# Hybrid delta-rule encoder on one core: the first norm's squares added in pairs on VectorE, layer 2 tiles from token 14, the scan's record in the inverse's tile, query-key blocks one tile sooner

## The chip, the cores and the metric

The kernel runs on one core of one Trainium2 chip. The metric is the device time of one execution in microseconds (us), lower is better. An execution takes 2422.28 us before the change (median of 3 runs, 2419.74 to 2425.08).

## The reference

Two layers of a hybrid encoder over 1040 tokens (16 learned meta tokens ahead of 1024 inputs) of width 1024, all in float32. The meta tokens are dropped at the end, so the second layer's outputs are only wanted from token 16 on.

```python
def hybrid_mixer(h, w_in, conv_qkv_w, a_log, dt_bias, dn_norm_w, sc_conv_w, w_out):
    proj = h @ w_in.astype(h.dtype)
    qkv, z, b_raw, a_raw, sc_b, sc_c, sc_h = jnp.split(proj, idx, axis=-1)
    qkv = jax.nn.silu(depthwise_conv_centred(qkv, conv_qkv_w))
    ...
    q = l2norm(q.reshape(Bsz, L, DN_HEADS, DN_HEAD_DIM))
    k = l2norm(k.reshape(Bsz, L, DN_HEADS, DN_HEAD_DIM))
    ...
    o_fwd = chunk_gated_delta_rule(qp, kp, vp, gp[:, :, 0], bp[:, :, 0])
    o_bwd = flip(chunk_gated_delta_rule(flip(qp), flip(kp), flip(vp),
                                        flip(gp[:, :, 1]), flip(bp[:, :, 1])))
    o = (o_fwd + o_bwd)[:, N_PAD:]
    ...
    y_sc = sc_b * depthwise_conv_centred(sc_c * sc_h, sc_conv_w)
    mix = jnp.concatenate([o, y_sc], axis=-1)
    return mix @ w_out.astype(h.dtype)

for l in range(DEPTH):
    h = h + hybrid_mixer(rmsnorm(h, norm1_w[l]), w_in[l], ...)
    h = h + swiglu(rmsnorm(h, norm2_w[l]), w_gate_up[l], w_down[l])
h = rmsnorm(h, final_norm_w)
return h[:, N_META:]
```

Each delta-rule group (4 heads of 128) needs, for each chunk and direction, the inverse of a unit triangular matrix made of key-key products and decays, a query-key block times the same decays, and then a scan over the chunks that carries a 128x128 state per head. The convolutions have three taps (one token to either side).

## The kernel before

**Layout.** The activations lie transposed: 128 channels on the partitions, tokens along the free axis. A projection of 1024 channels to a tile of 128 channels (`dense`) is 8 steps in k, and each step is three products, because an fp32 operand is held as a rounded high part and a low part: high x high (L169), high weight x low input (L170), low weight x high input (L171). The 1040 tokens go in three chunks of 348, 346 and 346, so a tile of 128 channels is 3 x 24 products; each chunk has a PSUM bank of its own and is evacuated by VectorE (L333 with the norm's factor `rstd` multiplied in, L338 as a plain copy). Weights come by DMA as `raw`, ScalarE makes the high part `whi` (L138), VectorE the low part `wlo` (L139).

**Order.** The program's order on each engine is set by a scheduler from priorities: the dense products of a layer run through, and small jobs are queued (`jobs`, `jobs2`, `jobs3`), of which one each is issued behind every chunk of 24 products. The tensor engine (PE) therefore sees a nearly unbroken row of dense products with small products let in between. "Dense product number n" below counts L169, L170 and L171 from the start of the program.

**First norm.** The squares of the 8 input tiles `hv` are summed over the partitions by products with a matrix of ones, column-tiled: four products of 128x32 with 260 tokens each lie side by side in one bank `fps` (L287). There are 8 x 4 of them, one set for each input tile. The root (L222), its reciprocal (L223) and two DMAs through DRAM (`rsd`, then `rstd` spread over the partitions) follow. The first two tiles of keys are evacuated before `rstd` is there, as copies, and multiplied later (L797).

**Attention of a layer.** In order: four key tiles (each: projection, convolution, silu, square, and a sum of squares over the channels by products with `sel`, L736), then the query tiles, the gates (L389, L426), the decays, which go to DRAM as `dtd` (L519), the key-key products, and the substitution that inverts 32x32 blocks (`sub_start`, `substitute`, in a tile with the halves `W` and `X`, VectorE L607 and L608). Then come four value tiles and, alternating, tiles of the short convolution (`sc_tile`) and of the output gate (`z_tile`). During those, `jobs2` holds `chunk_a` for each chunk: the query-key products (L573), two loads of decays `dt` from DRAM (issued by ScalarE's queue, L576), two multiplications on VectorE (L577), and two writes to `aqd` (L578, SP's queue). The `dt` tiles are from a ring of five buffers. The query-key banks are two. `jobs3` holds `invert`, which joins the 32x32 inverses to 128x128 ones in five rounds, `first` to `fifth` (L652 to L713). The fourth reads `W` last, the fifth reads `X` last.

**Scan.** Two directions run interleaved, each with a record of values `V`, keys `K`, query-key blocks `A` and gate `sz`, loaded from DRAM by SP's queue (L927 to L930; for the meta tokens L1008 and L1026). The record `rec` (L907) is a tile of its own that takes the buffer of the inverse's tile:

```python
rec = sb.tile([128, 4 * L], F32, tag=Y[0][2], name=nm("rec"))
```

Then come the output projection, the second norm and the feed-forward part (2816 channels), which take the rest of a layer's time.

## Time and profile before

| quantity | value |
|---|---|
| median of 3 runs | 2422.28 us |
| profiled execution, its own time | 2422.37 us |
| its span on the core | 2420.6 us |
| VectorE (DVE) busy | 1829.9 us |
| ScalarE (ACT) busy | 1045.7 us |
| GpSimd (POOL) busy | 70.3 us |
| mean DMA rate over the span | 139 GB/s |

The span runs from the first to the last recorded instruction; 1.8 us of the run's own time lie outside it. In the rows below, the first number is the start in us from the span's start and the second the busy time; "x8" counts instructions, and a bracket holds the idle time of the engine ahead of the row with what ended it. A product in float32 that is 32 columns wide, or one of 128x128, is recorded as two matmul records.

### The profile page before, as it was taken

The page shows a single profiled execution, that of the slowest core. Times are in us where ns is not written, and L with a number is a line of the kernel's source. Part 1 is how long each engine was busy: PE and PEld are TensorE (multiplying, and loading weights), DVE is VectorE, ACT ScalarE, POOL GpSimd, SP SyncE. Part 2 cuts the span into 40 slices and gives each one's busy share as a digit, 9 for nine tenths or more (in the row PEclk, how much of TensorE's full clock was granted, in tenths as well). Part 3 has the DMA queues.
Part 4 walks back from the last instruction along what each step waited for, and adds up shares of the span by engine and source line. Part 5 has one row for each costly group of instructions (what it writes and reads, how often), then busy time and mean ns, then how long its engine had stood idle before and what let it go on. Part 6 is the DMA issues. An engine that isn't in the chain of part 4 may idle for free.

```text
span 2420.6 us, 44960 instructions
## 1 busy us (share of the span) xinstructions
PE 2403.1 (99%) x17559; PEld 2228.1 (92%) x17559; DVE 1829.9 (76%) x3320; ACT 1045.7 (43%) x1977; POOL 70.3 (3%) x157
## 2 busy tenths in 40 slices
PE   9999999999999999999999999999999999999998
PEld 8999999999999999999999998998988888888887
DVE  6797545769888877977657985457898887778875
ACT  6653234446233333444446532335653343334444
POOL 0140000000000000000000200000000000000002
PEclk9999999999999999999999999999999999999999
DMA  4545344634222224674224444446433232347641
GB/s 136 158 154 187 119 154 150 206 111 132 93 97 89 102 74 136 224 246 148 89 84 151 154 154 145 147 144 222 142 114 113 77 112 85 121 144 249 204 127 70
DMA packets 202637, 336.60 MB, mean 139 GB/s; under 512 B 23488, under 2 KB 89208, under 8 KB 202424
## 3 DMA queue, kind: packets, MB, share of 16 engines
q1 hardware_dynamic: 174600, 295.12, 36.5%
q10 hardware_dynamic: 25648, 34.24, 4.3%
q0 software_dynamic: 2176, 4.36, 0.6%
q8 instruction: 138, 2.26, 0.4%
q14 instruction: 75, 0.61, 0.1%
HBM read 251.52 MB, written 82.12 MB: 138 GB/s over the span
## 4 chain that ended last, share of the span: by engine, by line
PE 95%; DMA 2%; DVE 2%; ACT 1%; SPq 0%; issue 0%; DVEq 0%; ACTq 0%
PE pacc L169 11%; PE pacc L170 11%; PE pacc L171 11%; PE pacc L1240 4%; PE pacc L1244 4%; PE pacc L1243 4%; PE pb L1244 3%; PE pb L1240 3%; PE pb L1243 3%; PE pf L940 3%; PE pf L1240 3%; PE pf L1244 3%; PE pf L1243 3%; PE pb L940 3%; PE pacc L1808 2%; PE pacc L1807 2%
## 5 line engine op out<-in xcount | busy, mean ns | idle before, releaser
L169 PE MATMUL pacc<-a,whi 128*128 128x346 f32 (+1 forms) x800 | 259.8, 325 | 0.6 <-ACT a L190 0.3
L171 PE MATMUL pacc<-a,wlo 128*128 128x346 f32 (+1 forms) x800 | 259.5, 326 | 0.2
L169 PE MATMUL pacc<-b,whi 128*128 128x346 f32 (+2 forms) x672 | 232.1, 346 | 0.4 <-ACT b L1124 0.3
L171 PE MATMUL pacc<-b,wlo 128*128 128x346 f32 (+2 forms) x672 | 231.6, 347 | 0.0
L138 ACT ACTIVATE whi<-raw 128x512 fp32r<-128x512 f32 x166 | 104.2, 630 | 285.0 <-PE pacc L170 206.3
L170 PE MATMUL pacc<-a,whi 128*128 128x346 f32 (+1 forms) x681 | 221.4, 325 | 0.6 <-DVE a L191 0.6
L170 PE MATMUL pacc<-b,whi 128*128 128x346 f32 (+2 forms) x580 | 199.4, 344 | 0.0
L169 PEld LDWEIGHTS pacc<-a,whi 128*128 128x128 f32 x800 | 151.0, 189 | 2.7 <-issue 1.1
L171 PEld LDWEIGHTS pacc<-a,wlo 128*128 128x128 f32 x800 | 150.8, 189 | 2.2 <-issue 1.3
L139 DVE TENSOR_TENSOR wlo<-raw,whi 128x512 fp32r<-128x512 f32 x166 | 113.8, 687 | 45.4 <-ACT whi L138 44.7
L169 PEld LDWEIGHTS pacc<-b,whi 128*128 128x128 f32 x672 | 126.3, 188 | 11.0 <-issue 1.3
L171 PEld LDWEIGHTS pacc<-b,wlo 128*128 128x128 f32 x672 | 126.1, 188 | 10.1 <-issue 2.3
L170 PEld LDWEIGHTS pacc<-a,whi 128*128 128x128 f32 x681 | 128.6, 189 | 3.8 <-issue 1.5
L170 PEld LDWEIGHTS pacc<-b,whi 128*128 128x128 f32 x580 | 109.1, 188 | 6.6 <-issue 0.6
L1222 ACT ACTIVATE whi<-rw 128x512 fp32r<-128x512 f32 (+1 forms) x84 | 51.7, 620 | 105.9 <-PE pacc L1243 27.4
L1222 ACT ACTIVATE b<-rw 128x512 fp32r<-128x512 f32 (+1 forms) x63 | 38.7, 620 | 89.2 <-PE pb L1243 34.5
L1222 ACT ACTIVATE a<-rw 128x512 fp32r<-128x512 f32 (+1 forms) x63 | 38.5, 619 | 71.9 <-PE pacc L1243 33.1
L1223 DVE TENSOR_TENSOR wlo<-rw,whi 128x512 fp32r<-128x512 f32 (+1 forms) x84 | 56.2, 671 | 6.5 <-ACT whi L1222 6.1
L333 DVE TENSOR_TENSOR a<-pacc,rstd 128x346 f32<-128x346 f32 (+2 forms) x59 | 32.6, 553 | 36.7 <-PE pacc L171 34.3
L1808 PE MATMUL pacc<-P,wlo 128*128 128x260 f32 (+1 forms) x177 | 59.4, 336 | 0.0
L1805 PE MATMUL pacc<-P,whi 128*128 128x260 f32 (+1 forms) x177 | 59.4, 336 | 0.0
L1807 PE MATMUL pacc<-P,whi 128*128 128x260 f32 (+1 forms) x177 | 59.4, 336 | 0.0
(1160 smaller groups left out, 7844.0 us busy)
## 6 DMA issues: line engine op xcount, KB each, us to landing
raw<-in_w_in SPq DMA_DIRECT2D x110, 256.0 KB
raw<-in_w_gu SPq DMA_DIRECT2D x106, 256.0 KB
rw<-in_w_gu SPq DMA_DIRECT2D x90, 256.0 KB
rw<-in_w_dn SPq DMA_DIRECT2D x90, 192.0 KB
rec<-vkd SPq DMA_DIRECT2D x61, 256.0 KB
raw<-in_w_out SPq DMA_DIRECT2D x48, 256.0 KB
b<-ad SPq DMA_DIRECT2D x45, 260.0 KB
a<-ad SPq DMA_DIRECT2D x45, 256.0 KB
```

The costliest lines, as they stand in the source:

```text
L138: whi_done[0] = hasten(wpr, lambda: act(out=hi, in_=raw[:, 0:kk, :], func=AF.Copy))
L139: whi_done[1] = hasten(wpr, lambda: tt(out=lo, in0=raw[:, 0:kk, :], in1=hi.bitcast(F32), op=ALU.subtract))
L169: mm(ps[:, :n], wh, xh[:, n0:n1], start=(i == 0), stop=False)
L170: mm(ps[:, :n], wh, xl[:, n0:n1], start=False, stop=False)
L171: last_mm[0] = mm(ps[:, :n], wl, xh[:, n0:n1], start=False, stop=(i == K - 1))
L940: one = mm(*args, **kw)
L1222: hasten(wpr, lambda: act(out=hi, in_=src, func=AF.Copy))
L1240: one = mm(ps[:, :CW], w[0][:, k, :], th[:, cs], start=first and k == 0, stop=False, skip_group_check=True)
L1243: mm(ps[:, :CW], w[0][:, k, :], tl[:, cs], start=False, stop=False, skip_group_check=True)
L1244: one = mm(ps[:, :CW], w[1][:, k, :], th[:, cs], start=False, stop=stop and k == nk - 1, skip_group_check=True)
L1807: mm(ps[:, :CW], wh[:, k, :], tl[:, cs], start=False, stop=False, skip_group_check=True)
L1808: mm(ps[:, :CW], wl[:, k, :], th[:, cs], start=False, stop=en, skip_group_check=True)
```

## The change

Four places change.

1. **First norm.** Each of four squares (ScalarE) gets a second one added to it (two of them squared by VectorE, two by ScalarE; the addition on VectorE), so four sets of column-tiled products are left instead of eight. The tie that held a set until its neighbour's squares were there goes.
2. **Layer 2 from token 14.** The query tiles and the first two parts of the short-convolution tiles are projected, convolved and multiplied from token 14 on, in three chunks of 342 (`near`). The squares of the query tiles are set to zero ahead of token 14 by GpSimd.
3. **The record lies in the inverse's tile by parts**, with the directions' halves exchanged, so a load into `W`'s half depends on `fourth` alone. The forward direction's meta tokens take the place of the other direction's `sz`.
4. **`chunk_a` is queued one tile sooner and `invert` one chunk sooner.** In layer 1 a third key tile is evacuated as a copy and multiplied later.

```diff
     sqs = big(S[1][0][2])
-    sqs = [sqs[:, i, :] for i in range(4)] + [c4k("sq") for _ in range(2)]
-    sqs += sqs[0:2]
+    sqs = [sqs[:, i, :] for i in range(4)]
...
     def first_sums():
-        order = (0, 4, 1, 5, 2, 6, 3, 7)
-        for i0 in (0, 2, 4, 6):
-            ready = [square(i, order[i]) for i in (i0, i0 + 1)]
-            for i in (i0, i0 + 1):
-                for j in range(4):
-                    one = mm(fps[32 * j:32 * j + 32, 0:260], ones[:, 0:32], sqs[i][:, 260 * j:260 * j + 260], start=(i == 0), stop=(i == KT - 1), skip_group_check=True)
-                    if i == i0 and j == 0:
-                        after(one, ready[1])
+        for i in range(4):
+            act(out=sqs[i], in_=hv[i], func=AF.Square)
+            more = c4k("sq")
+            if i < 2:
+                tt(out=more, in0=hv[i + 4], in1=hv[i + 4], op=ALU.mult)
+            else:
+                act(out=more, in_=hv[i + 4], func=AF.Square)
+            tt(out=sqs[i], in0=sqs[i], in1=more, op=ALU.add)
+            for j in range(4):
+                mm(fps[32 * j:32 * j + 32, 0:260], ones[:, 0:32], sqs[i][:, 260 * j:260 * j + 260], start=(i == 0), stop=(i == 3), skip_group_check=True)
...
+        o1 = 14 if last else 0
+        near = [(14, 356), (356, 698), (698, 1040)] if last else FULL
...
+            inv["all"] = tile_
...
         def lengths(which, q, row_, buf):
-            act(out=row_, in_=row_, func=AF.Silu)
-            act(out=buf, in_=row_, func=AF.Square)
+            o = o1 if which == "q" else 0
+            act(out=row_[:, o:L], in_=row_[:, o:L], func=AF.Silu)
+            if o:
+                nc.gpsimd.memset(buf[:, 0:o], 0.0)
+            act(out=buf[:, o:L], in_=row_[:, o:L], func=AF.Square)
...
-            late = pos < (2, 1)[l]
+            late = pos < (3, 1)[l]
...
-                inproj(i, to_row_late(t) if late else to_row(t))
+                inproj(i, to_row_late(t) if late else to_row(t), chunks=FULL if i >= 4 else near)
...
-            inproj(16 + 3 * i, to_row(t0))
-            tt(out=t0, in0=t0, in1=rstd, op=ALU.mult)
+            inproj(16 + 3 * i, to_row(t0), chunks=near)
+            tt(out=t0[:, o1:L], in0=t0[:, o1:L], in1=rstd[:, o1:L], op=ALU.mult)
...
-            inproj(17 + 3 * i, times(t0))
+            inproj(17 + 3 * i, times(t0), chunks=near)
...
-            if j == 1:
+            if j == 0:
                 jobs2.extend([lambda c=c: chunk_a(c) for c in ca])
             if j == 1:
-                jobs3.extend([None] * 7 + invert())
+                jobs3.extend([None] * 6 + invert())
...
-        rec = sb.tile([128, 4 * L], F32, tag=Y[0][2], name=nm("rec"))
+        rec = inv["all"]
...
-            base = d * 2048
+            base = (1 - d) * 2048
...
-            base = d * 2048
-            V, K = (rec[:, base + 512 * i:base + 512 * i + 128] for i in range(2))
+            base = (1 - d) * 2048
+            at_ = 1536 if d == 0 else base
+            V, K = (rec[:, at_ + 128 * i:at_ + 128 * i + 128] for i in range(2))
```

`conv` gets an argument `o`, from which token it works, and has otherwise the same three instructions. In the changed program the lines from L273 to L1000 stand one to four numbers lower or higher: L573, L576, L577 and L578 are L571, L574, L575 and L576 there, L621 is L620, L618 is L617, L389 is L387, L736 is L735, L333 is L331, L927 is L929.

How the order changes is shown at three places. First the tensor engine in layer 1 where the gate products are let in, between the projections of two key tiles (`pacc_550`, `pacc_661` before; `pacc_540`, `pacc_652` after). Before:

```order
L171 MATMUL pacc_550<-a_3_74,wlo_472 128x346
L389 MATMUL pb_582<-sel_184,P_37_212 128x16 x5
L736 MATMUL pf_515<-b_47_230,sel 32x260 x4
L389 MATMUL pb_582<-sel_184,P_37_212 128x16 x4
L169 MATMUL pacc_661<-a_1_72,whi_648 128x348
L170 MATMUL pacc_661<-a_2_73,whi_648 128x348
```

After, the gate products at that place:

```order
L171 MATMUL pacc_540<-a_3_74,wlo_462 128x346
L387 MATMUL pb_573<-sel_182,P_35_210 128x16 x9
L169 MATMUL pacc_652<-a_1_72,whi_639 128x348
L170 MATMUL pacc_652<-a_2_73,whi_639 128x348
L171 MATMUL pacc_652<-a_1_72,wlo_640 128x348
```

And behind 28 dense products more, the sums of the first key tile's squares (`b_45` there, `b_47` before):

```order
L171 MATMUL pacc_682<-a_1_72,wlo_640 128x346
L169 MATMUL pacc_682<-a_1_72,whi_639 128x346
L735 MATMUL pf_505<-b_45_228,sel 32x260 x4
L170 MATMUL pacc_682<-a_2_73,whi_639 128x346
L171 MATMUL pacc_682<-a_1_72,wlo_640 128x346
```

The sums are no longer among the gate products; they stand 28 dense products further on.

Second, ScalarE in layer 1 around the first loads of decays (`dt`) and the copies that pack the substitution's result (`P` from the inverse's tile `b_178`, `b_180` after). Before:

```order
L824 ACTIVATE b_251_2175<-b_251_2175 128x1040
L576 DMA dt_2264<-dtd_226 128x512
L576 DMA dt_2268<-dtd_226 128x512
L576 DMA dt_2303<-dtd_226 128x512
L621 ACTIVATE P_862<-b_178_1526 32x32x32 x4
L855 ACTIVATE b3f_2055<-pa_2130 128x512
L621 ACTIVATE P_863<-b_178_1526 32x32x32 x4
L138 ACTIVATE whi_2451<-raw_2453 128x512
L576 DMA dt_2307<-dtd_226 128x512
```

After:

```order
L826 ACTIVATE b_262_2211<-b_262_2211 128x1040
L857 ACTIVATE b_221_1931<-pa_2039 128x512
L858 DMA vkd_199<-b_221_1931 128x4x128
L620 ACTIVATE P_853<-b_180_1517 32x32x32
L574 DMA dt_2152<-dtd_224 128x512
L574 DMA dt_2156<-dtd_224 128x512
L620 ACTIVATE P_853<-b_180_1517 32x32x32 x3
L620 ACTIVATE P_854<-b_180_1517 32x32x32 x4
L574 DMA dt_2198<-dtd_224 128x512
L138 ACTIVATE whi_2481<-raw_2483 128x512
```

The first two loads stand behind the first packing copy instead of ahead of it, the third behind all eight. On the tensor engine the eight query-key blocks of layer 1 begin at dense products 984, 1086, 1086, 1113, 1113, 1136, 1147 and 1186 before, and at 912, 1084, 1108, 1116, 1130, 1142, 1184 and 1184 after; the first products of `first` (L652, L651 after) begin at 1200 and at 1184.

Third, SP's queue at the start of the scan in layer 1. Before:

```order
L826 DMA szd_199<-b_332_3020 128x1040
L137 DMA raw_3563<-in_w_in 128x512
L137 DMA raw_3650<-in_w_in 128x512
L927 DMA rec_4203<-vkd_201 128x512
L929 DMA rec_4203<-vkd_201 128x512
L930 DMA rec_4203<-aqd_202 128x512
```

After:

```order
L137 DMA raw_3548<-in_w_in 128x512
L929 DMA b_180_1517<-vkd_199 128x512
L931 DMA b_180_1517<-vkd_199 128x512
L1011 DMA b_180_1517<-vkd_199 128x1x128
L1029 DMA b_180_1517<-vkd_199 128x1x128
L828 DMA szd_197<-b_336_3061 128x1040
L932 DMA b_180_1517<-aqd_200 128x512
```

The first values and keys of both directions are issued ahead of the last gate tile's write, into the inverse's tile itself. The scan's first products stand behind dense product 1443 instead of 1465, and `fifth` behind 1416 instead of 1440.

18 lines of the change are left out of this document (7 added, 11 removed).

## The prediction

> **What bounds the kernel now.** I read the page's busy shares first, then the chain of work that ended last, then the tensor engine's waits.
>
> ```profile
> PE 2403.1 (99%) x17559; PEld 2228.1 (92%) x17559; DVE 1829.9 (76%) x3320; ACT 1045.7 (43%) x1977; POOL 70.3 (3%) x157
> ...
> PE 95%; DMA 2%; DVE 2%; ACT 1%; SPq 0%; issue 0%; DVEq 0%; ACTq 0%
> ```
>
> The tensor engine (PE) is busy 99% of the span and makes up 95% of the chain. So the change can help in two ways only: PE is given less to do, or one of its few waits goes. Work on VectorE (DVE), ScalarE (ACT) or GpSimd (POOL) costs nothing until PE waits for it.
>
> ```profile
> PE pb L573 <- DVE dt L577: 2.7, 2, 2.6
> PE pf L1018 <- DMA rec<-vkd: 1.3, 1, 1.3
> ...
> PE pf L736 <- ACT b L768: 0.7, 1, 0.7
> ```
>
> These are the PE waits (total, times, longest) that the change touches: 4.7 us together, all in layer 1. The sum is made against the profiled execution's 2422.4 us (its span and 1.8 us outside it), which stands 0.1 us above the median of the runs.
>
> **1. First norm.**
>
> ```profile
> 28.75 0.63 PE L287 MATMUL pb<-b,ones 128*32 128x260 f32 x4
> ...
> 30.46 0.65 PE L287 MATMUL pb<-sq,ones 128*32 128x260 f32 x8
> ...
> 33.94 2.51 PE L381 MATMUL pacc<-b,P 128*32 128x348 f32 x31
> ```
>
> PE has no idle time near these rows, so products taken out here count. A product is two records. Four records took 0.63 us and eight took 0.65: a short block is mostly the switch to 32-column tiles and back. These sums and the gate rows (L381) stand in five blocks among the dense products before and in five after, so I count no switch as saved, only length: 31 records of 348 columns took 2.51 us, 0.081 each. 32 records go: 2.6 us at that rate, 1.9 if it scales with the 260 columns. I take **-2.2**.
>
> DVE gets two squares and four additions for four squares, ACT six squares for four. That hides as long as the norm's factor comes in time:
>
> ```profile
> 43.50 1.25 DVE L797 TENSOR_TENSOR b<-b,rstd 128x1040 f32<-128x1040 f32 x1 [5.57 <-DMA rstd<-rsd]
> ```
>
> The last sums now stand 13 dense products (0.16 us each) and some 9 gate-row products (0.16) later in PE's row; less the 2.2 gained, everything from the root (L222) to `rstd` comes about 1.3 us later, `rstd` at 44.8 instead of 43.5. The third key tile is copied out instead of multiplied, so its banks don't wait for that; it costs DVE one more pass of 1.25 us. What is late next is the low weight part of the fourth key tile's second half: behind `rstd` DVE does three multiplications, three convolution passes (1.25 each) and two copies (0.5) before it, and its own 0.7, so it ends near 53.9, while PE, 2 to 3 us ahead of before, wants it at 54.7. The cover is 0.8 us. I take +0.5 for this and other small new waits in both layers (0 to +2).
>
> **2. The first sums of squares, and the clock.**
>
> ```profile
> 52.02 1.18 PE L389 MATMUL pb<-sel,P 128*128 128x16 f32 x10
> 53.92 0.65 PE L736 MATMUL pf<-b,sel 128*32 128x260 f32 x8 [0.72 <-ACT b L768]
> 54.50 1.24 PE L389 MATMUL pb<-sel,P 128*128 128x16 f32 x8
> 55.57 0.64 PE L169 MATMUL pacc<-a,whi 128*128 128x348 f32 x1
> ...
> 58.33 0.48 PE L169 MATMUL pacc<-a,whi 128*128 128x348 f32 x1
> 58.62 0.35 PE L170 MATMUL pacc<-a,whi 128*128 128x348 f32 x1
> 58.81 0.32 PE L171 MATMUL pacc<-a,wlo 128*128 128x348 f32 x1
> 58.97 0.32 PE L169 MATMUL pacc<-a,whi 128*128 128x348 f32 x1
> ```
>
> PE waits 0.72 us for the first tile's squares. After, these sums stand 28 dense products later (4.5 us), while the squares come some 1.3 to 2 us later and PE some 3 us sooner: about 1 us of cover. The wait goes: **-0.7**. From 55.57 on the 348-column products start 0.29 us apart (58.33 to 58.62), from 58.81 on 0.16: eleven products took 3.05 us instead of some 1.7. So 1.4 us went to a granted clock that fell after 3.5 us of light work. After, only the gate products are left there, 2.2 us. I expect the clock to hold, at three chances in four: **-1.0** (0 to -1.4).
>
> The Trainium skill ("TensorE: Matmul & The Clock Gate", section "HAM oscillation — how this bites in real kernels") has the rule that gaps of more than about 3.4 us without PE work lower the clock. The rows differ: the only gap here is 0.72 us, and the rest of the stretch is small products. By the rule alone nothing in the change would move the clock, and this term would be 0.
>
> **3. Layer 2 from token 14.**
>
> ```profile
> 2099.72 0.28 PE L1652 MATMUL pacc<-a,b 128*128 128x256 f32 x1
> 2099.84 0.28 PE L1653 MATMUL pacc<-a,b 128*128 128x256 f32 x1
> 2099.96 0.39 PE L1240 MATMUL pb<-a,whi 128*128 128x512 f32 x1
> 2100.19 0.40 PE L1243 MATMUL pb<-a,whi 128*128 128x512 f32 x1
> ```
>
> Products of 256 columns start 0.12 us apart and of 512 columns 0.23: 0.43 ns for a column, so nothing else sets their pace at these widths. Twelve tiles (four queries, eight of the short convolution) lose 14 columns in 24 products each: 12 x 24 x 14 x 0.43 ns = **-1.7** (0 if the pace were not by columns, but the rows exclude that). Four memsets on POOL are new. Each waits for the buffer's last reader, and behind them in POOL's queue stand the keys' norm loads, on which DVE's key multiplications and then the key-key products hang. No row shows a memset there; POOL's mean instruction is 70.3/157 = 0.45 us, and a late one could cost PE some tenths, which the +0.5 above holds.
>
> **4. The record in the inverse's tile.**
>
> ```profile
> 297.96 0.33 SPq L927 DMA_DIRECT2D rec<-vkd  x1
> ```
>
> The record's first load is issued at 297.96, right behind `fifth`; L1018 then waits 1.25 us and L940 0.2 us for such loads. In the new tile the loads that the first step and the meta step need go to the half that `fourth` frees, two chunks of dense products (48 x 0.16 = 7.7 us) earlier, more than the waits. **-1.4** (0 to -1.45). Late next is the copy of `fifth`'s result; the scan has 27 dense products behind `fifth` instead of 25, so that is covered as before. In SP's queue a gate tile's write now stands behind the waiting loads; nothing in layer 1's scan reads it for several steps.
>
> **5. Query-key blocks and the inverse sooner.** This is the unsure term.
>
> ```profile
> 215.60 4.27 ACT L621 ACTIVATE P<-b 32x1024 f32<-32x1024 f32 x4 [7.06 <-DMA dt<-dtd]
> ...
> 212.16 4.04 DVE L619 STREAM_TRANSPOSE b<-b 128x1024 f32<-128x1024 f32 x2
> 222.68 0.61 DVE L577 TENSOR_TENSOR dt<-pb,dt 128x512 f32<-128x512 f32 x1
> ...
> 243.36 0.68 DVE L577 TENSOR_TENSOR dt<-pb,dt 128x512 f32<-128x512 f32 x1
> ...
> 237.27 1.13 PE L573 MATMUL pb<-b,b 128*128 128x128 f32 x8 [2.57 <-DVE dt L577]
> 244.44 1.06 PE L573 MATMUL pb<-b,b 128*128 128x128 f32 x8
> ...
> 225.00:240.00 15.00, 12.20 (x83) 11.25 (x82) 8.69 (x13) 2.08 (x4) 0.00 (x0) 1.00 0.94 308
> ```
>
> The eight blocks go through two banks, so block n needs the multiplications of block n-2; those go through a ring of five `dt` buffers, each filled and emptied by DMA. From 225 to 240 us the DMA share is 0.94 at 308 GB/s: the ring is paced by transfers. PE waits 2.57 us at the seventh block, and the eighth (244.44) starts 0.4 us after the sixth block's last multiplication (243.36 + 0.68).
>
> After, the seventh and eighth blocks both stand at dense product 1184, where the eighth stood at 1186. Without the waits PE is there 2.74 + 0.3 us sooner against the substitution's end, at 241.4 on the old time. At the old ring's pace it would wait 2.6 us until 244.04: the wait is only moved. The ring also starts later: its first loads stand behind a packing copy (212.16 + 2 + 1.1 = 215.3) and the second block's first load behind all eight (222.8, and some 2.7 us to land), where that block was multiplied at 222.68. That is 2.8 us more if nothing is caught up; fewer transfers then compete, so I count a bit less than half: a wait of 3.7 instead of 2.7, **+1.0**. Bounds: -2.7 (no wait is left) and +10.5 (below).
>
> **Sum.** -2.2 + 0.5 - 0.7 - 1.0 - 1.7 - 1.4 + 1.0 = -5.5, so 2422.4 - 5.5 = 2416.9 us. Less than 0.2% (4.8 us) is about what a measurement of this kernel can't tell from no change.
>
> **The rivals.**
>
> *The ring's wait goes whole* (-2.7 instead of +1.0): 2413.2. For it: blocks one to four are asked for over 46 dense products instead of in pairs, which spreads the transfers. Against it: the late start. Chance 0.2.
>
> *The ring becomes the bound: slower.* The place is the eighth block at dense product 1184. The full delay of the second block's load is 222.8 - 215.6 = 7.2 us, and ahead of the fifth block's multiplications DVE now has both transposes and their copies (6.8 us, half of which stood behind it before): 3.4. If neither is caught up, the wait grows by 10.6 us, and the time is 2422.4 - 6.5 + 10.5 = 2426.4. It is slower than before once the wait at these blocks is above 2.7 + 6.5 = 9.2 us. Against it: DVE was idle for some 5 us between these multiplications before. Chance 0.08.
>
> *The factor's lateness and the clock.* If `rstd` comes 2 us later still, the wait at the first sums returns with another at the low weight part, and the clock falls as before: +0.7 + 1.0 + 1.5, giving 2420.1. For it: a cover of about 1 us in two places. Chance 0.17.
>
> *The clock is as it was.* The slow products from 55.57 on came from something that the change leaves, and the term is 0: 2417.9. Against it: they begin right behind the light stretch, and nowhere else. Chance 0.05. This is where the rule of the Trainium skill leads.
>
> *The change doesn't do what it says*: the record's loads still wait behind others in SP's queue, and the shorter sums leave the switches (-1.9): 2422.4 - 5.5 + 1.4 + 0.3 = 2418.6. Chance 0.1; the forecast keeps 0.4.
>
> **How the numbers follow.** The forecast spreads about 2 us either way, across the 2417.4 that bounds "faster". A little over half of it (0.22), nearly all of the first rival (0.19) and a fifth to a third of the last three (0.09) lie below: faster 0.5. The slower rival lies above 2427.2 in about half its cases: slower 0.05. The rest is within: 0.45. The range reaches from 2411, the first rival with 2 us less, to 2421.5, which leaves out the slower rival and the worst of the third.
>
> **What the changed profile would show.** L285 with 32 records and the same number of blocks; no wait at L735, and a clock of 1.00 from 50 to 60 us; 342-column products about 2 ns closer; no wait for the record; and the waits at L571 by DVE L575, whose sum decides between the first two rivals. The forecast is wrong if those waits exceed 6 us, if PE waits for a weight part near 54 us, or if layer 2 has a new wait at the key-key products.

## The result and the profile after

The change makes the kernel a little slower, where the forecast was 5.5 us faster.

| | before | after |
|---|---|---|
| median, in runs that alternate on one chip | 2423.44 us (9 runs, 2419.74 to 2426.36) | 2430.75 us (9 runs, 2428.08 to 2432.28) |
| ratio to before, 95% interval | 1 | 1.0028 [1.0018, 1.0039] |
| span of the profiled execution | 2420.6 us | 2426.1 us |

The page of the changed kernel, its busy shares and its chain of work:

```profile
PE 2403.8 (99%) x17527; PEld 2226.6 (92%) x17527; DVE 1834.8 (76%) x3323; ACT 1051.1 (43%) x1979; POOL 71.0 (3%) x161
...
PE 93%; DMA 2%; DVE 2%; ACT 1%; issue 1%; POOL 1%; SPq 0%; ACTq 0%; DVEq 0%; POOLq 0%
```

PE runs 32 records fewer and is busy 0.7 us longer. The chain shows the same turn: PE's share falls from 95% to 93%, so waits make up more of the chain. The tensor engine's waits, with total, number and longest in us:

```profile
PE pb L571 <- DVE dt L575: 2.4, 3, 1.3
PE pacc L171 <- DVE wlo L139: 2.0, 2, 1.3
PE pacc L169 <- ACT ptm L515: 1.9, 1, 1.9
...
PE pa L856 <- ACT a3f L857: 0.8, 1, 0.8
...
PE pf L735 <- ACT b L770: 0.5, 1, 0.5
```

The wait for the record and the 0.7 us at the first sums of squares are gone. The block wait is there again (2.4 for 2.7), and there are new waits: for weight parts, for an evacuation behind the decays, for a transpose's input.

To find where time goes I use one ruler throughout: the start of the n-th dense projection product (lines L169 to L171) on PE, in this kernel and in the kernel before. Both have the same 5,664 of them in the same order, so the difference is a running balance. Small jobs are placed differently between them, so I cut where both have, but for one product of 16 columns, the same jobs behind them. These are us gained (-) or lost (+) per stretch, worked out from the two PE timelines, beside the terms of the prediction that fall there:

| dense products | where | forecast | after |
|---|---|---|---|
| 0 to 384 | first norm, key tiles (to 87 us before) | -3.9 | -4.1 |
| 384 to 816 | query tiles, decays (to 171 us) | +0.5 | +7.3 |
| 816 to 1440 | substitution, query-key blocks, inverse (to 298 us) | +1.0 | +2.1 |
| 1440 to 1536 | first scan steps (to 324 us) | -1.4 | -1.9 |
| 1536 to 2688 | rest of layer 1 | 0 | -0.1 |
| 2688 to the last | layer 2's projections and scan | -1.7 | +2.0 |
| sum | | -5.5 | +5.3 |

The start won what was forecast. It was lost again at once, and layer 2 shows the wrong sign. The start first, PE's timeline where the slow clock stood before (55 to 59 us):

```profile
50.37 2.08 PE L387 MATMUL pb<-sel,P 128*128 128x16 f32 x18
52.30 0.40 PE L169 MATMUL pacc<-a,whi 128*128 128x348 f32 x1
52.54 0.32 PE L170 MATMUL pacc<-a,whi 128*128 128x348 f32 x1
52.70 0.32 PE L171 MATMUL pacc<-a,wlo 128*128 128x348 f32 x1
```

Right behind the gate products, products of 348 columns start 0.24 and then 0.16 us apart: no wait, and the granted clock is 1.00. Now PE 40 us later:

```profile
92.55 0.46 PE L169 MATMUL pacc<-a,whi 128*128 128x348 f32 x1 [1.86 <-ACT ptm L515]
93.47 1.10 PE L735 MATMUL pf<-b,sel 128*32 128x260 f32 x8 [0.47 <-ACT b L770]
...
97.86 0.49 PE L169 MATMUL pacc<-a,whi 128*128 128x348 f32 x1
98.15 0.49 PE L170 MATMUL pacc<-a,whi 128*128 128x348 f32 x1
...
99.58 0.32 PE L170 MATMUL pacc<-a,whi 128*128 128x346 f32 x1
99.73 0.32 PE L171 MATMUL pacc<-a,wlo 128*128 128x346 f32 x1
```

Two waits, 2.3 us, and behind them 0.29 us from one product to the next (97.86 to 98.15) until 99.6. The same stretch by windows (start, length, busy time and count of PE, PEld, DVE, ACT, POOL; granted clock, DMA share, GB/s):

```profile
88.00:96.00 8.00, 5.67 (x32) 4.30 (x31) 5.28 (x19) 6.52 (x10) 0.00 (x0) 0.80 0.72 264
96.00:104.00 8.00, 8.00 (x44) 8.00 (x43) 8.00 (x22) 4.22 (x7) 1.05 (x2) 0.78 0.80 249
```

The clock fall that the change removed at 55 us has its like at 93 us, twice as long: by the trace's clock records 6.8 us at half speed instead of 3.4. Waits and slow products together are the 5.4 us that dense products 384 to 480 lose.

Who is late there? The engines around the first decays, after (an engine's name with a "q" is its queue issuing a transfer; `gd` holds the gates' cumulative products in DRAM, `ptm` is a tile of decays in the making):

```profile
82.17 0.39 SPq L433 DMA_DIRECT2D gd<-P  x1
...
82.54 1.10 POOL L457 DMA_DIRECT2D bc<-rnd  x2
...
84.78 2.87 ACTq L512 DMA_DIRECT2D ptm<-gd  x6
...
90.72 1.25 DVE L514 SCALAR_TENSOR_TENSOR ptm<-ptm,nGb,off 16x16 f32<-16x16 f32 x8 [4.46 <-DMA ptm<-gd]
...
91.90 0.50 DVE L331 TENSOR_TENSOR b<-pacc,rstd 128x348 f32<-128x348 f32 x1
```

and before:

```profile
75.73 0.34 SPq L435 DMA_DIRECT2D gd<-P  x1
...
78.96 1.31 ACTq L514 DMA_DIRECT2D ptm<-gd  x3
...
80.52 1.24 DVE L516 SCALAR_TENSOR_TENSOR ptm<-ptm,nGb,off 16x16 f32<-16x16 f32 x8 [1.41 <-DMA ptm<-gd]
```

The gates' cumulative products, which these decays start from, stand 48 dense products further on in PE's row (343 instead of 295). So they are written at 82.2 instead of 75.7. The loads of the decays' inputs are issued 5.8 us later, and then take 5.9 us until DVE can start (84.78 to 90.72), where they took 1.6. DVE sits idle 4.46 us for them, and behind them in its order stands the evacuation (L331) for whose bank PE waits. The profile's row for PE names ACT L515, which comes last by its records; DVE's row shows the evacuation ending at 92.40 and PE starting at 92.55.

### The profile page after: what moved, and what is told of

The parts are those of the page before. It is cut to its first block, busy times and chain, and to the rows that moved or that the text cites. A ratio compares the mean times of both kernels' runs of the same rounds, so it can differ in the third digit from the quotient of the medians.

```text
span 2426.1 us, 44913 instructions
## 1 busy us (share of the span) xinstructions
PE 2403.8 (99%) x17527; PEld 2226.6 (92%) x17527; DVE 1834.8 (76%) x3323; ACT 1051.1 (43%) x1979; POOL 71.0 (3%) x161
## 4 chain that ended last, share of the span: by engine, by line
PE 93%; DMA 2%; DVE 2%; ACT 1%; issue 1%; POOL 1%; SPq 0%; ACTq 0%; DVEq 0%; POOLq 0%
PE pacc L169 10%; PE pacc L171 10%; PE pacc L170 10%; PE pacc L1243 4%; PE pacc L1247 4%; PE pacc L1246 4%; PE pb L1247 3%; PE pb L1243 3%; PE pb L1246 3%; PE pf L942 3%; PE pf L1243 3%; PE pf L1247 3%; PE pf L1246 3%; PE pb L942 3%; PE pacc L1811 2%; PE pacc L1810 2%
## 5 line engine op out<-in xcount | busy, mean ns | idle before, releaser
L169 PE MATMUL pacc<-a,whi 128*128 128x346 f32 (+1 forms) x800 | 260.5, 326 | 3.1 <-ACT ptm L515 1.9
L171 PE MATMUL pacc<-a,wlo 128*128 128x346 f32 (+1 forms) x800 | 259.2, 325 | 2.1 <-DVE wlo L139 2.0
L169 PE MATMUL pacc<-b,whi 128*128 128x342 f32 (+3 forms) x672 | 232.1, 346 | 0.0
L171 PE MATMUL pacc<-b,wlo 128*128 128x342 f32 (+3 forms) x672 | 231.2, 346 | 0.0
L170 PE MATMUL pacc<-b,whi 128*128 128x342 f32 (+3 forms) x580 | 198.7, 343 | 0.0
L169 PEld LDWEIGHTS pacc<-a,whi 128*128 128x128 f32 x800 | 151.2, 189 | 4.5 <-ACT ptm L515 2.1
L171 PEld LDWEIGHTS pacc<-a,wlo 128*128 128x128 f32 x800 | 150.9, 189 | 4.7 <-DVE wlo L139 3.0
L171 PEld LDWEIGHTS pacc<-b,wlo 128*128 128x128 f32 x672 | 126.4, 188 | 10.2 <-issue 2.3
L169 PEld LDWEIGHTS pacc<-b,whi 128*128 128x128 f32 x672 | 126.4, 188 | 9.8 <-issue 1.5
L331 DVE TENSOR_TENSOR a<-pacc,rstd 128x342 f32<-128x342 f32 (+3 forms) x59 | 32.5, 550 | 43.1 <-PE pacc L171 42.8
```

The source lines that it names most:

```text
L169: mm(ps[:, :n], wh, xh[:, n0:n1], start=(i == 0), stop=False)
L170: mm(ps[:, :n], wh, xl[:, n0:n1], start=False, stop=False)
L171: last_mm[0] = mm(ps[:, :n], wl, xh[:, n0:n1], start=False, stop=(i == K - 1))
```

## The experiments

Each kernel ran in five rounds against the kernel before on the same chip. Variants are made from the kernel before or the changed one; a diff shows what differs from it, with "..." for lines left out. Ratios are to before, with the 95% interval. The stretches of the profiles are collected in one table behind the runs; each is one execution and carries some us of chance (below), so whole kernels are compared by the ratios.

### Is it the evacuation behind the decays? (e1)

The first group of decays is queued one place later, and its subtractions are held until the evacuation ahead of them is done.

```diff
-                    stt(out=gr[0:n, h, 0:n], ...)
+                    one = stt(out=gr[0:n, h, 0:n], ...)
+                    if c == 0 and l == 0:
+                        after(one, evacs[-1])
...
-                jobs2.extend([None, None, lambda: chunk_g(0), None])
+                jobs2.extend([None, None, None, lambda: chunk_g(0)])
```

> The changed kernel with one more order on VectorE in layer 1: the first evacuation of the second query tile stands ahead of the decay multiplications of the meta chunk, not behind them. Nothing is left out. Theory A (the gates come 48 dense products later, so the decays' loads land late, VectorE waits for them with an evacuation queued behind, PE waits 1.9 us for that bank at 90.7 us and 0.5 us at the next sums, and the clock falls for 6.8 us behind these waits): the 1.9 us wait goes, the clock holds or falls less, and the time is 4 to 6 us below the changed kernel's (about 2425 to 2426.5). Rival B (the loss of 5 us between dense products 384 and 480 is work or DMA that only shows at this wait): the wait comes back at the next evacuation or at the next weight part, and the time stays within 1.5 us of the changed kernel.

1.0027 [1.0018, 1.0035], as slow as the change. PE's timeline, the rows with the longest waits there:

```profile
91.77 0.65 PE L737 MATMUL pf<-b,sel 128*32 128x260 f32 x8 [0.87 <-ACT b L772]
...
95.93 0.43 PE L169 MATMUL pacc<-a,whi 128*128 128x348 f32 x1 [1.41 <-ACT whi L138]
...
125.49 0.65 PE L737 MATMUL pf<-b,sel 128*32 128x260 f32 x8 [2.45 <-ACT b L772]
```

The 1.86 us are gone and the clock didn't fall here, but PE now stands at the next items in its row: two sums of squares and a high weight part. Removing one wait didn't remove the loss: from 384 to 816 e1 loses 8.5 us.

### Undoing parts of the change (e2, e3, e4)

The first norm as before (its old `square` and `order` loop); all tokens in layer 2 (with the last short-convolution multiplication over all tokens too); part 4's queueing undone (the third key tile stays late):

```diff
-    sqs = [sqs[:, i, :] for i in range(4)]
+    sqs = [sqs[:, i, :] for i in range(4)] + [c4k("sq") for _ in range(2)]
+    sqs += sqs[0:2]
```

> The changed kernel with the first norm as before (eight sets of sums, no additions on VectorE), the other parts kept. The gates then stand at dense product 297 instead of 343. Theory A: the stretch from dense 384 to 480 takes as long as before (16.9 us, not 22.4), the early gain of 4.6 us at dense product 288 falls to about 1 us, so the whole is within 2 us of the changed kernel (about 2429 to 2431). Rival C (the later gates come from the third key tile's copy, not from the pairs): the stretch still takes over 20 us, and the time rises to about 2434.

```diff
-        o1 = 14 if last else 0
-        near = [(14, 356), (356, 698), (698, 1040)] if last else FULL
+        o1 = 0
+        near = FULL
...
```

> The changed kernel with layer 2's tiles from token 0 again. In the profiles layer 2's attention took 2.0 us more than before where 1.6 us less were due by the columns. Theory D (the new chunks shift layer 2's order, which brings the two waits of 0.8 and 0.7 us and 1 to 2 us of small gaps): the time falls by about 2 us against the changed kernel (about 2428.5). Rival E (the sooner query-key blocks bring them): the time rises by the columns' 1.6 us (about 2432).

```diff
-            if j == 0:
+            if j == 1:
...
-                jobs3.extend([None] * 6 + invert())
+                jobs3.extend([None] * 7 + invert())
```

> The changed kernel with the query-key blocks and the inverse queued as late as before. Theory E: layer 2's waits at the value transposes and the finalising transposes go (1.5 us) and with them 1 to 2 us of small gaps; layer 1's waits at the query-key blocks go back from 2.4 us and the neighbouring 1.6 us to the 2.7 us of before; the time is 3 to 4 us below the changed kernel (about 2427). Rival D: layer 2 stays as slow as in the changed kernel, and the time is within 1.5 us of it.

e2: 1.0043 [1.0030, 1.0055]. e3: 1.0047 [1.0034, 1.0059]. Undoing either part doesn't make the kernel faster, so neither alone holds the loss. By the medians the parts would be worth some 4 us each inside the change, but both intervals overlap with the change's, so that isn't shown. e4: 1.0004 [0.9995, 1.0013]: with the blocks and the inverse where they were, the loss is nearly gone.

### Is VectorE's total work the cause? (e5, e6)

In layer 1, half of the decays' subtractions are left out: two of the four heads lack them, in the changed kernel (e5) and in the kernel before (e6).

```diff
-                for h in range(H):
+                for h in range(H if l else 2):
```

> The changed kernel with half of layer 1's decay subtractions left out (two of four heads, about 9 us of VectorE between 80 and 140 us). Theory F: from dense product 384 to the end of the substitution VectorE's chain (decays, key norm, key-key blocks, substitution, 100 to 215 us) sets the pace, so PE's lead of 4.6 us at dense 288 is lost there. With less of that work the substitution ends 4 us or more sooner, PE keeps most of its lead to dense 1104, and the time falls 4 to 8 us against the changed kernel. Rival G (the lead is lost to single late loads and ScalarE's queue, not to VectorE's sum of work): the waits at 91 and 124 us stay, and the time falls by less than 2 us.

> The kernel before with the same work left out. Theory F: before, PE has no wait in this stretch and is just level with VectorE, so PE gains nothing up to dense 1104; only the wait of 2.6 us at the query-key blocks may shrink: the time falls 0 to 2.5 us. Rival (VectorE's work is passed to PE in the kernel before too): the time falls by 4 us or more.

e5: 1.0044 [1.0031, 1.0057]; e6: 1.0016 [1.0008, 1.0024]. e6 is slower than before with less work, e5 no faster than the change. In e5 the substitution ended 5 us sooner (207.8 instead of 212.9 us), and yet, by PE's waits:

```profile
PE pf L735 <- ACT b L770: 5.5, 3, 3.8
```

PE waits 5.5 us at the sums of squares, for rows that are squared by ACT. So DVE's sum of work isn't the bound; what is left is the order in which things come ready.

### Parts alone on the kernel before (e7, e8, e12, e15)

Parts 2 and 3 together; the pairs alone; the third key tile's copy alone; the record alone. Their lines are those of the change; for e12 and e15 they are short:

```diff
-            late = pos < (2, 1)[l]
+            late = pos < (3, 1)[l]
```

```diff
-        rec = sb.tile([128, 4 * L], F32, tag=Y[0][2], name=nm("rec"))
+        rec = inv["all"]
...
-            base = d * 2048
+            base = (1 - d) * 2048
...
```

> The kernel before with parts 2 and 3 of the change only (layer 2 from token 14, the record in the inverse's tile). Both lie outside the stretch in which the lead is lost. Prediction's terms: -1.7 and -1.4, so 3 us below before (ratio 0.9987). If the record's wait only moves or layer 2 is bound by something else than PE, one of the two is missing: -1.5 or 0.

> The kernel before with part 1's pairs alone (two late key tiles as before). Theory F: PE is 4 to 5 us ahead at dense 240 and has lost it by dense 816; the gates stand at dense 322, so the time is 0 to 4 us above before. By the prediction's terms (-2.2, -0.7, -1.0, +0.5) it would be 3.4 us below.

> The kernel before with the third key tile's copy alone. The gates stay at dense product 297, but one more pass on VectorE and another order of the sums follow. Theory H: any shift of this order against the scheduler's own times brings PE waits between dense 384 and 816: 3 to 8 us above before, as with the pairs alone (e8). Rival: without later gates there is no loss, and it is level with before within 1.5 us.

> The kernel before with the record in the inverse's tile alone. The prediction's term: -1.4 (ratio 0.9994), by the waits for the record that go. If the token part is what ate that gain in e7, this one keeps it.

e15: 0.9994 [0.9985, 1.0003], 1.4 us below before's median, though the interval holds no change too; its stretch 1440 to 1536 gives -1.8. e7: 1.0004 [0.9995, 1.0014]: the record's stretch gives its -1.8, but layer 2 loses 2.2 in all, with a new wait at the key-key products in the profile:

```profile
PE pb L528 <- DVE a L462: 1.3, 1, 1.3
```

The same wait in layer 2, 1.9 us, stands in the profile of e13 (below), which has neither part, so it isn't shown to come from them.

e8: 1.0020 [1.0011, 1.0028], e12: 1.0030 [1.0020, 1.0039]. Each alone makes the kernel slower, e12 with no gain at the start at all. PE's timeline of e8 and of e12, the longest wait of each:

```profile
105.45 1.10 PE L735 MATMUL pf<-b,sel 128*32 128x260 f32 x8 [3.77 <-ACT b L770]
```

```profile
162.59 0.63 PE L169 MATMUL pacc<-a,whi 128*128 128x348 f32 x1 [4.41 <-DVE b L335]
163.02 0.49 PE L170 MATMUL pacc<-a,whi 128*128 128x348 f32 x1
163.31 0.49 PE L171 MATMUL pacc<-a,wlo 128*128 128x348 f32 x1
```

Other items are late in each, 57 us apart, and behind both waits the clock is halved (in e12 0.29 us from product to product; the clock records show 6.827 us of it in both). e2, which has e12's order of the sums, has e12's wait too: 3.92 us at 163.3.

The rows of e12 show where its wait comes from, though no run tests it alone. SP's queue in e12, with what hangs on its weight load:

```profile
157.37 0.27 SPq L552 DMA_DIRECT2D m0d<-mt  x1
157.75 0.33 SPq L137 DMA_DIRECT2D raw<-in_w_in  x1
...
160.41 0.63 ACT L138 ACTIVATE whi<-raw 128x512 fp32r<-128x512 f32 x1 [8.96 <-DMA raw<-in_w_in]
...
161.08 0.69 DVE L139 TENSOR_TENSOR wlo<-raw,whi 128x512 fp32r<-128x512 f32 x1 [4.78 <-ACT whi L138]
```

and the same two transfers before:

```profile
143.77 1.28 SPq L137 DMA_DIRECT2D raw<-in_w_in  x1
...
150.90 0.28 SPq L550 DMA_DIRECT2D m0d<-mt  x1
```

In e12 the weight load stands behind the write of `m0d`, the small inverse for the meta tokens, which POOL finishes at 157.3; before, the same load stood ahead of that write. So the load goes 14 us later, DVE waits 4.78 us for the weight part made from it, and behind that in DVE's row stands the evacuation for whose bank PE waits 4.41 us.

### Giving the late items more room (e9, e10)

e1, and the sums of the first and third query tile 37 and 45 dense products later; e10 has the blocks and the inverse back as in e4.

```diff
-            jobs.append(lambda: sums(which, q, buf))
+            jobs.extend(([None] * 3 if l == 0 and which == "q" and q in (0, 2) else []) + [lambda: sums(which, q, buf)])
```

> The changed kernel with the evacuation of e1 first and with the sums of the first and third query tile's squares 37 and 45 dense products later in PE's row (layer 1). Nothing is left out. Theory H (PE's row is strict: the loss between dense 384 and 816 is PE standing at single small products whose ScalarE work is queued behind the decays that came late, and the clock that falls behind such a wait): the waits of 0.9 and 2.5 us at these sums go, dense 816 is reached 3 to 4 us sooner than in e1, and the time falls 3 to 5 us against the changed kernel (ratio to before about 1.001). Rival I (the stretch is bound by VectorE and ScalarE as a whole): PE stands at the next item instead, and the time is within 1.5 us of the changed kernel (1.0028).

> As e9, with the query-key blocks and the inverse queued as late as before. If theory H holds and the sooner blocks cost 5 to 6 us by themselves (e4), both gains add: 3 to 5 us below before (ratio about 0.9985). If the two share one cause, it stays level with before, as e4.

e9: 1.0039 [1.0025, 1.0054]; e10: 0.9999 [0.9990, 1.0007]. In e9 the sums no longer wait, and up to 126 us PE's waits are at two other items:

```profile
94.47 0.42 PE L169 MATMUL pacc<-a,whi 128*128 128x346 f32 x1 [2.12 <-DVE b L331]
...
125.89 0.33 PE L466 MATMUL pa<-ident,b 128*128 128x128 f32 x1 [1.95 <-ACT kt L469]
```

The rise from e10 to e9, 0.4%, is again the blocks and the inverse together; e18 below parts them.

### Blocks or inverse? (e11, e13, e14, e17)

On the kernel before: both sooner (e11), the blocks alone (e13: `j == 0` for `chunk_a`), the inverse alone (e14: `[None] * 6`). On the changed kernel: only the inverse back (e17).

```diff
-                jobs3.extend([None] * 7 + invert())
+                jobs3.extend([None] * 6 + invert())
```

> The kernel before with part 4's sooner query-key blocks and inverse alone. From e4 against the changed kernel: 5 to 6 us above before (ratio 1.0024), in layer 1 by waits at the blocks and at the inverse's first round (dense 1104 to 1440), in layer 2 by waits at transposes. The prediction's term: +1.0, ratio 1.0004.

> The kernel before with the query-key blocks alone queued a tile sooner; the inverse stays. The last two blocks stand at dense products 1193 and 1200, the first round of the inverse at 1200; the first decay loads stand where they stood, the third behind all eight packing copies. Theory J (the ring of decay tiles starts later and PE asks for the last blocks no later, so PE waits for the ring): a wait of 3 us or more at the last two blocks with the clock falling behind it, 3 to 6 us above before (ratio 1.0015 to 1.0025). Rival K (the inverse's sooner place does it): level with before within 1.5 us.

> The kernel before with the inverse alone queued a chunk sooner (first round at dense 1180 with the last block beside it). Rival K: the loss of e11 shows here, 3 us or more above before, by a wait inside the first round. Theory J: the wait at the seventh block stays at 2 to 3 us, at most 1.5 us more is waited inside the first round, and the time is level with before within 2 us.

> The changed kernel with only the inverse put back one chunk of dense products later; the query-key blocks stay a tile sooner. Theory K (the inverse's place is what part 4 costs): ratio 1.000, as when blocks and inverse were both put back. Rival (the blocks cost something among the other parts, though not alone): 1.002 or more.

e11: 1.0043 [1.0030, 1.0057]. e13: 0.9994 [0.9985, 1.0003]. e14: 1.0028 [1.0017, 1.0040]. e17: 1.0010 [1.0001, 1.0019]. Alone, the blocks cost nothing that these runs show; the inverse, one chunk sooner, costs 0.28% alone and by the medians about 0.18% in the changed kernel (1.0028 to 1.0010, intervals that touch). PE's timeline of e14, at the seventh block of layer 1 and in the inverse's first round of layer 2:

```profile
239.68 1.13 PE L575 MATMUL pb<-b,b 128*128 128x128 f32 x8 [3.44 <-DVE dt L579]
...
241.29 0.49 PE L170 MATMUL pacc<-a3f,whi 128*128 128x346 f32 x1
241.58 0.49 PE L171 MATMUL pacc<-a,wlo 128*128 128x346 f32 x1
```

```profile
1467.14 1.13 PE L575 MATMUL pb<-a,a 128*128 128x128 f32 x8 [0.24 <-DVE dt L579]
1468.20 0.31 PE L655 MATMUL pf<-e,P 32*32 32x32 f32 x20
1471.39 1.13 PE L575 MATMUL pb<-a,a 128*128 128x128 f32 x8 [2.87 <-DVE dt L579]
1472.44 1.02 PE L655 MATMUL pf<-e,P 32*32 32x32 f32 x88
```

and DVE ahead of that block:

```profile
1470.55 0.69 DVE L579 TENSOR_TENSOR dt<-pb,dt 128x512 f32<-128x512 f32 x1 [2.96 <-DMA dt<-dtd]
```

The inverse's first round is issued in two halves, each recorded as 128 small products (L655, 32x32). Queued a chunk sooner, the first half meets the last blocks, which go into the middle of it (x20, block, x88), with no dense products between them. In layer 2 of e14 PE waits 2.87 us there, while DVE's block multiplication waits 2.96 us for a load of decays. In layer 1 of e14 most of the loss stands elsewhere: at the seventh block, still ahead of the round, PE waits 3.44 us where it waited 2.57 before, and there the clock fell for 3.4 us. That this comes from the inverse isn't shown; the clock also fell at these blocks in e15, whose inverse is where it was. In the changed kernel layer 1 has blocks inside the round too:

```profile
246.62 1.13 PE L571 MATMUL pb<-b,b 128*128 128x128 f32 x8 [0.60 <-DVE dt L575]
247.68 0.26 PE L651 MATMUL pf<-e,P 32*32 32x32 f32 x6
248.42 1.13 PE L571 MATMUL pb<-b,b 128*128 128x128 f32 x8 [0.48 <-DVE dt L575]
249.48 1.17 PE L651 MATMUL pf<-e,P 32*32 32x32 f32 x114
```

and with only the inverse back (e17):

```profile
246.31 1.05 PE L571 MATMUL pb<-b,b 128*128 128x128 f32 x8
...
249.12 1.06 PE L571 MATMUL pb<-b,b 128*128 128x128 f32 x8
...
251.06 1.29 PE L651 MATMUL pf<-e,P 32*32 32x32 f32 x128
```

Dense products lie between the blocks again, neither of these waits is there, and each half of the round runs in one piece.

### Looking for a faster version (e16, e18)

e16 is the kernel before with the blocks sooner and the record (its lines as above); e18 is e9 with the inverse back.

> The kernel before with two parts alone: the query-key blocks a tile sooner (inverse where it was) and the scan's record in the inverse's tile. Each alone stood level with the kernel before, at 0.9994. Theory M (what each part saves in its own profile survives in the whole): 1.3 us from the record's waits and next to nothing from the blocks, ratio 0.999. Rival N (a saving of this size is lost at the next wait): 1.000.

> The changed kernel with the first evacuation ahead of the decays, the sums of squares of the first and third query tile about 40 dense products later, and the inverse back one chunk later; the blocks stay a tile sooner. With the blocks also put back it stood at 0.9999. Theory K: 1.000, and if the blocks' earlier transfers spare the ring's wait of 1.6 us, 0.9993. Rival: the blocks' transfers delay others, 1.002.

e16: 0.9993 [0.9984, 1.0002]. e18: 1.0007 [0.9999, 1.0016]. Neither is shown to be faster than before; no variant was. But e18 and e9 (1.0039 [1.0025, 1.0054]) differ by the inverse's place alone, and their intervals don't touch: this is the clearest price of the inverse inside the change.

### The stretches of all profiles

Us lost (+) or gained (-) against the profile of before, by the same ruler ("N" pairs in the first norm, "L" third key tile late, "T" tokens from 14, "R" record, "A" blocks sooner, "I" inverse sooner):

| run | has | 0-384 | 384-816 | 816-1440 | 1440-1536 | 1536-2688 | 2688-end | ratio |
|---|---|---|---|---|---|---|---|---|
| after | N L T R A I | -4.1 | +7.3 | +2.1 | -1.9 | -0.1 | +2.0 | 1.0028 |
| e1 | N L T R A I, evacuation first | -3.9 | +8.5 | +2.1 | -1.9 | -0.1 | +1.6 | 1.0027 |
| e5 | N L T R A I, half the decays | -4.2 | +9.9 | +1.3 | -1.9 | 0.0 | +3.5 | 1.0044 |
| e9 | N L T R A I, sums later | -4.5 | +7.7 | +3.6 | -1.9 | -0.1 | +2.6 | 1.0039 |
| e2 | L T R A I | +0.4 | +8.9 | -1.0 | -3.2 | +1.4 | +3.2 | 1.0043 |
| e3 | N L R A I | -3.9 | +10.2 | +1.4 | -1.9 | +0.2 | +7.3 | 1.0047 |
| e4 | N L T R | -4.5 | +8.8 | -2.3 | -3.5 | +4.2 | -1.2 | 1.0004 |
| e17 | N L T R A | -3.6 | +9.0 | -2.0 | -3.5 | +5.2 | -1.7 | 1.0010 |
| e10 | N L T R, sums later | -3.5 | +4.0 | -2.0 | -3.5 | +3.8 | -1.2 | 0.9999 |
| e18 | N L T R A, sums later | -4.1 | +8.7 | +0.7 | -3.6 | +2.3 | -1.0 | 1.0007 |
| e8 | N | -2.7 | +8.5 | 0.0 | -0.2 | +0.6 | +1.1 | 1.0020 |
| e12 | L | +0.4 | +9.2 | -2.4 | -0.5 | +0.8 | -0.2 | 1.0030 |
| e7 | T R | -1.3 | +0.8 | -0.8 | -1.8 | +1.6 | +2.2 | 1.0004 |
| e15 | R | +0.2 | +0.6 | +1.0 | -1.8 | +1.5 | +1.5 | 0.9994 |
| e16 | R A | -1.3 | +1.5 | +0.2 | -1.8 | +1.2 | +1.5 | 0.9993 |
| e13 | A | +1.3 | +0.9 | +0.2 | -0.1 | +0.1 | +2.3 | 0.9994 |
| e14 | I | -0.1 | +1.0 | +4.0 | -0.3 | +1.1 | +7.8 | 1.0028 |
| e11 | A I | +0.4 | +1.5 | +3.8 | -0.6 | 0.0 | +2.3 | 1.0043 |
| e6 | half the decays | -1.8 | +4.2 | +0.5 | -0.6 | +0.3 | +1.4 | 1.0016 |

At two cuts the jobs aren't the same: in e4, e10, e17 and e18 the scan starts later in PE's row, so 16 of its records (some 2 us, at 1.05 us for eight of 128x128) stand behind 1536 instead of ahead of it, and in e2 16 records more stand ahead of 1440. There the columns on both sides are to be read together.

From 384 to 816, every run with N or L loses 7 to 10 us (e10, with the sums later, 4.0), and every one without 0.6 to 1.5, apart from e6, which leaves work out (4.2).

The inverse's place is harder to find in the profiles. From 816 to 1440 e17 is 4.1 us better than the changed kernel, and they differ only in I. But it gives 3.7 of these back up to 2688: its PE waits 3.1 us there (1.28 at L1088 is the longest), the changed kernel's 0.6. So over the rest of layer 1 the two differ by 0.4 us, and e18 and e9 by 2.2. In layer 2 these pairs differ by 3.7 and 3.7. On the kernel before, e14 loses 4.8 us in layer 1 from 816 on and 7.8 in layer 2, but e11 loses in layer 2 no more than e13, which lacks I (2.3 each). The profiled runs lie apart from their medians: e14's took 2436.57 us (median 2431.33), e11's 2429.64 (2434.17), e13's 2427.32 (2424.18). That the inverse costs rests on the ratios; where it costs is only partly seen.

## Why the prediction was wrong

**Terms 1 and 2 were right, up to their end.** The first norm gave 1.8 us by dense product 144 (forecast 2.2), the first sums' wait went, and the clock held from 50 to 60 us: 4.1 us by product 384 for 3.9 forecast.

**The step that failed first is "I take +0.5 for this and other small new waits in both layers (0 to +2)".** It looked for lateness at one weight part near 54 us, where PE didn't wait, and it priced other lateness by that cover. The third key tile's copy was in it as one pass of DVE and no wait of PE. Measured is +7.3 us from 384 to 816. In the changed kernel PE came some 4 us earlier to work that other engines prepare, while the gates' cumulative products, and with them the decays, came 48 dense products later. The trace of before has no PE wait above 0.1 us between 54 and 226 us, which I read as slack; e8 and e12 show that the pairs alone, and the third key tile's copy alone, turn it into waits of 3.8 and 4.4 us, behind which the clock falls. (In e12 PE isn't early and the gates' products move by two dense products only, so these aren't the only seeds: there a weight load came to stand behind POOL's late write in SP's queue.) Less work on DVE didn't make it smaller (e5: +9.9), so it doesn't come from DVE's sum of work. That one item alone causes it is refuted: with each remedy (e1, e9) the next item in PE's row was late. Why the decays' loads took 5.9 us to land instead of 1.6 wasn't isolated: weight loads, the two key-norm loads (L457) and further decay loads on the same queue (six issued from 84.78 on, three from 78.96 before) ran at the same time, but no run moved these away.

**The second is term 5, "+1.0".** The range up to +10.5 held the truth, but the mechanism was put in the wrong place. I looked at the ring's pace and at the blocks, and never weighed `invert`'s one chunk as an edit of its own. The blocks alone cost nothing (e13). The inverse costs 6.8 us by the ratio of e14, some 4 in the changed kernel by the medians (e17) and some 8 between e18 and e9; the +1.0 held none of it. In the profiles part of it shows in layer 2, where I had no cost at all. In layer 2 the place where it shows differs: 2.87 us at a block in e14, 0.68 and 1.40 at two in e11; in the changed kernel no block waits there, and part of the 3.7 us against e17 is a wait of 0.84 for a transposed input (L856), though e15, without the inverse's move, has such a wait of 1.06 too. What sets the rest is open.

**The rival "the ring becomes the bound"** came nearest in time (2426.4) by luck, with a wrong sum: the wait at the blocks is 2.4 us, not above 9.2, so its condition wasn't met. Nor did any of the three signs come that the prediction named as its refutation (those waits above 6 us, a weight part near 54 us, key-key products in layer 2); what came were waits that no step named.

**Terms 3 and 4 show in their own stretches, not in the whole.** Term 4, the record: -1.4 forecast, -1.8 in the stretch and 1.4 us in the median of e15, whose interval still holds no change. Term 3, layer 2's columns: -1.7 forecast, -1.0 to -1.7 in layer 2 of the four profiles that have it and not the inverse's move (e4, e10, e17, e18); undoing it (e3) costs 0.19%, though the intervals of e3 and the change overlap. With the inverse sooner, layer 2 gives it all back. Together, on the kernel before (e7), the two were forecast at -3.1 us and gave +1.0, with an interval from -1.2 to +3.4: waits elsewhere took what they won.

**The sum by ratios.** Built up from before, parts 2 and 3 give +1.0 us (e7), part 1 with the late key tile adds nothing to that (e4 is at +1.0 too) where -3.4 was forecast, and part 4's queueing adds 5.8 us (e4 to the change) where +1.0 was forecast. Each difference is uncertain by some 3 us, but all three fall on the side of the loss: by these medians no part kept its forecast.

**The clock.** The prediction set the rows against the rule of the Trainium skill ("TensorE: Matmul & The Clock Gate", section "HAM oscillation — how this bites in real kernels") that idle gaps of more than about 3.4 us lower the clock. In the changed kernel the clock fell right behind a gap of 1.86 us, so by this trace shorter waits can suffice; not each does (in e1 it held behind 2.45 us). Another sentence of the page agrees: its section "What's actually happening" gives a free-running window of 3413 ns, and each spell at half speed in these profiles, apart from their ends, lasted 3.413 or 6.827 us by the trace's clock records. The times between two spells are whole windows too (27.307 us in e18, eight of them). I expected the clock to hold since its old trigger went; it held there and fell elsewhere, behind a new wait.

## What to carry to other kernels

When the bounding engine is 99% busy and hardly waits, read every edit that makes it faster, or that shifts a small job in its row, as a question to all the engines behind it: for each item in the next 100 us, when does it come ready and when is it asked for? An absence of waits in a profile is no slack; here either of two small edits at the start lost 8 us and more in the stretch behind it, for at most 3 us won, and made the whole slower by 0.2 and 0.3%. And add the balance up to the end: a gain in one stretch can be given back in the next. Look along the queues too: in e12 a weight load that came to stand behind a late write cost PE 4.4 us. Price each number that an edit changes by itself: of two numbers in one part, one alone cost nothing and the other 0.28%.

## What the runs showed of the hardware

A wait of PE costs more than its length: at waits of 0.5 to 4.4 us among small products, the dense products often ran at half speed for 3.413 or 6.827 us, which cost up to some 3 us more (the changed kernel lost 5.4 us where it waited 2.3). Less work on VectorE made the kernel before slower (e6, 0.16%); why wasn't isolated. And e10 and e18, whose work stands in the same order on PE up to dense product 889, lost 4.0 and 8.7 us from 384 to 816: the one had a slow spell of 3.4 us there, the other two. So a single profile of this kernel doesn't measure a stretch to better than some 4 us; the common sign over many does.
